# A diffusion backbone on one core: fetching each weight twice in place of splitting a raw copy

## The chip, the cores and the metric

The kernel runs on one core of a Trainium2 chip. The metric is device microseconds of one execution, the median of three runs; a profiled execution, recorded apart from these, gives the trace. TensorE (PE) multiplies matrices, VectorE (DVE), ScalarE (ACT) and GpSimd (POOL) work elementwise, SyncE (SP) issues transfers here, and 16 DMA engines carry them.

## The reference

Two layers over 256 context tokens and 256 latent tokens, 1024 channels, all in float32. Each layer is two normalised sub-layers with modulation: three parallel token mixers, then a gated MLP.

```python
def layer(x, ctx):                       # cut to what matters here
    u = rms_norm(x) * (1 + scale) + shift
    u_A, u_B, u_C, u_G = split_cols(u @ w_in)
    y = [rwkv7_branch(u_A), rglru_branch(u_B), na_branch(u_C)]
    m = sum(sigmoid(u_G[i]) * (y[i] @ w_branch[i]) for i in range(3))
    x = x + gate * rms_norm(m @ w_out)
    h = modulate(rms_norm(x))
    g, v = split(h @ ffn_w_in)
    return x + gate2 * rms_norm((silu(dwconv3(g)) * v) @ ffn_w_out)
```

Branch A is a recurrence (RWKV-7, in both directions), B a linear recurrence with gates, C attention in a neighbourhood. The second layer needs the outputs of the latent tokens alone.

## The kernel before

The tokens lie along the free axis, 512 of them (or 256 in the second layer's products of latent tokens), the channels in tiles of 128 on the partitions. Every large matrix product is made of three: operands are split into a high part, rounded to float32r, and a low part that holds the rest, and `mm3` (L240) adds high x high, low x high and high x low for each 128 x 128 block of the weight (L246, L247, L248).

A weight is a [128, 1024] tile, 512 KB (some of `ffn_w_out` have 768 columns). `wload` (L217) fetches it and splits it: a DMA from SP's queue into `wr` (L222), a ScalarE copy that rounds it into the high part `wh` (L225), and a subtraction raw less high into the low part `wl` (L228), on VectorE or GpSimd as a table for each phase says (L226). There are 402 such weights in an execution. The main pool `wp` has three places for raw tiles and two for each part; a low-rank weight `lw` (L464) shares the places of the raw tiles. Merges and MLP add a second pool with one to three places of each kind, and `phase` (L211) sets how the weights rotate between the two.

The order of work: in each layer a mixer part of eight head pairs, in which the recurrence of one pair (L713 to L747) runs beside the projections (`proj`, L252) for the next and beside B and C; then the merge of the three branches (`merge_w`, L1103), the output projection, and the MLP (`ffn_in` and `out`). Some of the second half's products run by halves of the tokens, 256 columns each. A planner orders each engine's instructions when the program is built, by priority and by what is ready in its own model of time, and sets the semaphore waits; on the chip each engine's queue then runs in that order, so that an instruction that waits holds up what is behind it on its engine. GpSimd's share of the recurrence is the decay of the state (`r`, L732), the key scaling (`n`, L487) and other small steps.

Of the kernel before, what the change touches and what calls it, by code (L numbers as in the profile page):

```python
# [10 lines left out]
F32 = mybir.dt.float32  # L11
F32R = mybir.dt.float32r
# [7 lines left out]
P = 128  # L20
NTOK = 512
CT = 8
NCH = 8
# [28 lines left out]
# per layer: the order in which a head pair's parts are traced, their priorities, how the products of the other  # L52
# mixers are spread beside them, and which engine takes the work that several could take
# [104 lines left out]
class Net:  # L158
# [51 lines left out]
    # ---- weights: raw -> (hi, lo) in float32r  # L210
    def phase(self, l, name, wps=None):  # L211
        """From here on the weights rotate among wps; where their low parts are worked out: 1 for GpSimd."""
        self.lo, self.wn = CFG[l]["lo"][name], 0
        if wps:
            self.wps, self.wi = wps, 0

    def wload(self, ap, kt):  # L217
        nc = self.nc
        pool = self.wps[self.wi % len(self.wps)]
        self.wi += 1  # L220
        raw = pool.tile([P, 1024], F32, tag="wr", name="wr", bufs=3 if pool is self.wp else None)[:, :kt * P]
        nc.sync.dma_start(raw, ap)  # L222
        hi = pool.tile([P, 1024], F32R, tag="wh", name="wh")[:, :kt * P]
        lo = pool.tile([P, 1024], F32R, tag="wl", name="wl")[:, :kt * P]
        nc.scalar.activation(hi, raw, AF.Copy)  # L225
        eng = nc.gpsimd if self.lo[self.wn % len(self.lo)] else nc.vector  # L226
        self.wn += 1
        eng.tensor_tensor(lo, raw, hi.bitcast(F32), op=ALU.subtract)  # L228
        return hi, lo
# [35 lines left out]
    # ---- rms statistics of the tokens a ... b - 1: acc holds the sums of squares over the channel tiles  # L265
# [15 lines left out]
    def stat(self, st, sq, a, b, first, last):  # L281
        """Adds the sums of sq over its channels to st, a column for 128 tokens."""
# [13 lines left out]
    # ---- conditioning vectors of a layer: mod[128, 48, 2]  # L296
# [16 lines left out]
    def ada_chunk(self, l, n, kind="c"):  # L313
        """Columns 512 n ... 512 n + 511 of the modulation, four column groups side by side on TensorE."""
# [22 lines left out]
        # modulation: h = x rstd (ng (1 + sc)) + sh ; x += (g ng) o rstd  # L337
# [12 lines left out]
    def layer_consts(self, l):  # L350
# [19 lines left out]
        # softplus(-lam) = max(-lam, 0) + log1p(exp(-|lam|)); log1p(u) = 2 atanh(u / (2 + u))  # L370
# [53 lines left out]
    # ---- A: RWKV-7  # L424
# [16 lines left out]
    def rw_start(self, Q):  # L441
# [4 lines left out]
        # stacked over the partitions: (hi, lo) of w, (lo, hi) of a  # L446
# [14 lines left out]
    def rw_key(self, R, Q, p, n0):  # L461
        nc = self.nc
        T2 = self.rw_t2(R, Q)
        lw = self.wp.tile([P, 1024], F32, tag="wr", name="lw", bufs=3)[:, :640]  # L464
# [12 lines left out]
        # normalised key  # L477
# [93 lines left out]
    def rw_gram(self, R, u, n0):  # L571
        nc = self.nc
        KR, BK = u["KR"], u["BK"]
        G = R.tile([P, 2, 2, 2, NCH, 64], F32, tag="Gm", name="Gm")  # part, d, h, c
# [22 lines left out]
    def rw_rows(self, R, u, n0):  # L597
# [3 lines left out]
        # from here on [beta; k] decayed to the end of its chunk  # L601
# [3 lines left out]
        # value rows by token, for both directions  # L605
# [12 lines left out]
        # rows by token of [beta; k]  # L618
# [13 lines left out]
    def rw_inv(self, R, u):  # L632
# [9 lines left out]
        if self.cfg['f1']:  # L642
            # the block beside them makes room for the rows of keys
# [10 lines left out]
        # columns s of the inverse: rows 0-63 hold the odd ones, rows 64-127 the even ones, both in the even places  # L654
# [16 lines left out]
    def rw_inv2(self, R, u):  # L671
# [4 lines left out]
        T1 = Ap  # rows 0-31: T11, rows 96-127: Q  # L676
# [134 lines left out]
    # ---- B: RG-LRU  # L811
# [16 lines left out]
    def lru_gates(self, B, u, d):  # L828
# [4 lines left out]
        if self.cfg['lq']:  # L833
            # the parts of the products lie where the second direction's values come
# [54 lines left out]
    # ---- C: neighbourhood attention  # L889
    def softmax(self, C, ps, nk):  # L890
        """ps: list of PSUM views [128, nk] (same width); returns normalised probabilities in SBUF."""
# [22 lines left out]
    def attn_qkv(self, C, p, n0):  # L914
# [13 lines left out]
        # values: 4 windows of 4 rows by 32 columns, then the context  # L928
# [8 lines left out]
    def attn_pre(self, C, u, n0):  # L937
        nc = self.nc
        q, k, vw = u["q"], u["k"], u["vw"]
        # queries by blocks (n, r, c): rotated, then plain  # L940
# [8 lines left out]
        if self.cfg['sq']:  # L949
            # (hi, lo) of a head's plain queries over the partitions, the high parts in the head's own half; the  # L950
            # high parts of the context's keys in both halves, the low ones beside each other
# [24 lines left out]
        # value rows by token: 4 windows, then 2 context tiles  # L976
# [9 lines left out]
    def attn_stages(self, C, u, n0):  # L986
        """The products of the attention in an order in which each finds its operands ready when
        other products stand between."""
# [68 lines left out]
    def attn_o(self, C, u, w, lat):  # L1057
        """Both heads side by side on TensorE's columns."""
# [32 lines left out]
    # ---- merging  # L1091
# [13 lines left out]
    def merge_w(self, M, tiles, ths, x, first, n0, ada=()):  # L1105
        """M += (1 + tanh(u_g / 2)) (y @ w) of a branch, twice the gated product."""
# [16 lines left out]
    def resid(self, S, l, o, acc, s, a, b, src, dst):  # L1123
        """x += gg * o * rstd(o) in the place of o; writes x to dst, and returns the sums of its squares."""
# [18 lines left out]
    def mixers(self, l, n0, src):  # L1143
# [7 lines left out]
        with ExitStack() as es:  # L1151
# [7 lines left out]
            with tc.high_priority(offset=30000):  # L1159
                if n0:  # L1160
                    # the products of the latent tokens alone go first
                    self.rw_gl(R, n0)
                    for _ in range(ng[0] - fg):
                        self.gate(B, next(gates), n0)
# [22 lines left out]
            for p in range(CT):  # L1187
# [3 lines left out]
                for o in order:  # L1191
# [11 lines left out]
                    with ExitStack() as z:  # L1203
                        if o == "A":
                            z.enter_context(tc.high_priority(offset=early))
                        # z: the pair whose recurrence is to come (the next one after T when nothing is left)
# [68 lines left out]
            # two branches merge beside the last head pair's recurrence, in the places of tiles done with  # L1275
# [42 lines left out]
    def btiles(B, n0):  # L1318
        """Tiles hi, lo of the 8 channel tiles in the places of the branches' tiles."""
# [275 lines left out]
```

## Time and profile before

| what | us |
|---|---|
| median of three runs | 3066.45 |
| lowest and highest | 3055.29, 3069.74 |
| span of the profiled execution, first to last instruction | 3050.6 |
| TensorE busy | 2886.2 (95%) |
| VectorE busy | 1968.9 (65%) |
| ScalarE busy | 1411.1 (46%) |
| GpSimd busy | 840.6 (28%) |

The span is shorter than the time of a run, since what lies before the first and after the last instruction isn't in it; the profiled execution has no time of its own beside its span. A matmul's record is longer than its step in the pipeline, so TensorE's busy time joins overlapping records. Busy time is a mean over very different parts of the kernel, which is why the stretches are read one by one.

### The profile page before, as it was taken

What the parts mean: (1) busy time and instruction counts of PE and PEld (TensorE: products, weight loads), DVE (VectorE), ACT (ScalarE), POOL (GpSimd) and SP (SyncE); (2) the same over time, 40 slices, a digit from 0 to 9 for tenths busy, and PEclk for the clock granted to TensorE, in tenths of its full rate; (3) what the DMA queues carried; (4) which work ended last, traced back from release to release, by engine and by line L of the source; (5) the groups of instructions that cost most, each with busy time, mean ns of one, the idle gap of its engine ahead of it and who ended that gap; (6) DMA issues with size and microseconds to landing.
All of it is one profiled execution on the core that took longest, in us unless ns stands there. A gap on an engine that the chain in (4) does not pass through costs nothing. (4 is left out here: it accounts for less than half of the span.)

```text
span 3050.6 us, 53179 instructions
## 1 busy us (share of the span) xinstructions
PE 2886.2 (95%) x21104; PEld 2265.9 (74%) x21104; DVE 1968.9 (65%) x3745; ACT 1411.1 (46%) x2485; POOL 840.6 (28%) x788
## 2 busy tenths in 40 slices
PE   7999999999999999999999998998999999998998
PEld 5666776766767678687778886776776777788898
DVE  6757658576686653465444267788677778775784
ACT  4454455554455452253323245454554545554553
POOL 3341322424234225100000113433432433414220
PEclk9999999999999899998999998998988999999899
DMA  6222122211222225755562352222222122245653
GB/s 229 81 70 67 59 71 66 74 60 56 69 76 70 84 100 180 273 190 180 198 223 92 107 183 82 62 78 69 68 72 69 62 70 78 77 140 205 222 188 115
DMA packets 130553, 344.39 MB, mean 113 GB/s; under 512 B 14720, under 2 KB 41600, under 8 KB 130304
## 3 DMA queue, kind: packets, MB, share of 16 engines
q1 hardware_dynamic: 123392, 334.69, 33.1%
q10 hardware_dynamic: 6912, 6.29, 0.7%
q8 instruction: 166, 2.72, 0.4%
q14 instruction: 83, 0.68, 0.1%
HBM read 301.08 MB, written 25.17 MB: 107 GB/s over the span
## 5 line engine op out<-in xcount | busy, mean ns | idle before, releaser
L225 ACT ACTIVATE wh<-wr 128x1024 fp32r<-128x1024 f32 (+1 forms) x402 | 420.8, 1048 | 581.0 <-PE pj L247 209.1
L248 PE MATMUL pj<-hh,wl 128*128 128x512 f32 (+1 forms) x1440 | 559.0, 389 | 41.4 <-DVE wl L228 40.0
L246 PE MATMUL pj<-hh,wh 128*128 128x512 f32 (+1 forms) x1440 | 569.7, 397 | 5.8 <-ACT gt L1088 3.0
L228 DVE TENSOR_TENSOR wl<-wr,wh 128x1024 fp32r<-128x1024 f32 (+1 forms) x310 | 398.2, 1285 | 266.5 <-ACT wh L225 244.2
L247 PE MATMUL pj<-hl,wh 128*128 128x512 f32 (+1 forms) x1440 | 556.0, 386 | 0.0
L228 POOL TENSOR_TENSOR wl<-wr,wh 128x1024 fp32r<-128x1024 f32 (+1 forms) x92 | 221.1, 2403 | 637.1 <-ACT wh L225 343.6
L248 PEld LDWEIGHTS pj<-hh,wl 128*128 128x128 f32 x1440 | 280.7, 195 | 104.6 <-DVE wl L228 45.7
L246 PEld LDWEIGHTS pj<-hh,wh 128*128 128x128 f32 x1440 | 280.6, 195 | 70.0 <-issue 16.4
L247 PEld LDWEIGHTS pj<-hl,wh 128*128 128x128 f32 x1440 | 280.4, 195 | 55.1 <-issue 13.4
L666 DVE TENSOR_TENSOR AT<-AT,itmp 128x126 f32<-128x126 f32 (+22 forms) x496 | 154.7, 312 | 11.8
L732 POOL TENSOR_TENSOR r<-SV,gC 64x256 f32<-64x256 f32 x96 | 84.2, 877 | 242.0 <-DVE SV L745 139.8
L664 DVE TENSOR_TENSOR itmp<-AT 128x126 f32<-128x126 f32 (+22 forms) x496 | 138.1, 278 | 12.0
L585 PEld LDWEIGHTS gram<-KR,BK 64*128 64x128 f32 x1024 | 116.3, 193 | 27.4 <-ACT Gm L590 14.8
L585 PE MATMUL gram<-KR,BK 64*128 64x128 f32 (+1 forms) x1024 | 131.3, 288 | 4.9 <-ACT Gm L590 4.7
L246 PE MATMUL fo<-fh,wh 128*128 128x256 f32 (+1 forms) x418 | 131.0, 313 | 0.0
L248 PE MATMUL fo<-fh,wl 128*128 128x256 f32 (+1 forms) x418 | 130.7, 313 | 0.0
L247 PE MATMUL fo<-fl,wh 128*128 128x256 f32 (+1 forms) x418 | 130.4, 312 | 0.0
L246 PE MATMUL fu<-hh,wh 128*128 128x256 f32 (+1 forms) x384 | 126.2, 330 | 3.1 <-DVE fgs L1347 2.4
L246 PE MATMUL fg<-hh,wh 128*128 128x256 f32 (+1 forms) x384 | 127.2, 333 | 0.1
L248 PE MATMUL fu<-hh,wl 128*128 128x256 f32 (+1 forms) x384 | 126.4, 330 | 0.8 <-DVE wl L228 0.8
L247 PE MATMUL fg<-hl,wh 128*128 128x256 f32 (+1 forms) x384 | 126.0, 330 | 0.0
L247 PE MATMUL fu<-hl,wh 128*128 128x256 f32 (+1 forms) x384 | 125.8, 328 | 0.0
(344 smaller groups left out, 6481.6 us busy)
## 6 DMA issues: line engine op xcount, KB each, us to landing
wr<-in_w_in SPq DMA_DIRECT2D x180, 512.0 KB, 3.2
aw<-in_ada_w SPq DMA_DIRECT2D x96, 512.0 KB, 4.4
wr<-in_ffn_w_in SPq DMA_DIRECT2D x96, 512.0 KB, 3.4
wr<-in_w_branch SPq DMA_DIRECT2D x48, 512.0 KB, 3.3
wr<-in_ffn_w_out SPq DMA_DIRECT2D x36, 512.0 KB, 3.5
wr<-in_w_out SPq DMA_DIRECT2D x24, 512.0 KB, 4.4
Gm<-KR SPq DMA_DIRECT2D x32, 256.0 KB, 3.6
wr<-in_ffn_w_out SPq DMA_DIRECT2D x18, 384.0 KB, 3.1
```

Source lines behind the costliest of these rows:

```text
L225: nc.scalar.activation(hi, raw, AF.Copy)
L228: eng.tensor_tensor(lo, raw, hi.bitcast(F32), op=ALU.subtract)
L246: nc.tensor.matmul(o, lhsT=a, rhs=xh[k][:, n0:n1], start=(first and k == 0), stop=False)
L247: nc.tensor.matmul(o, lhsT=a, rhs=xl[k][:, n0:n1], start=False, stop=False)
L248: m = nc.tensor.matmul(o, lhsT=b, rhs=xh[k][:, n0:n1], start=False, stop=(last and k == kt - 1))
L585: nc.tensor.matmul(ps[:, i, 0:nx], lhsT=BK[hs, d, c, :], rhs=KR[hs, 0:nx, d, c, :], start=True, stop=True)
L664: eng.tensor_tensor(tmp, Ap[:, q + 1:32, q:q + 1].to_broadcast([P, nt, ns]), Tf[:, q:q + 1, 0:2 * ns:2].to_broadcast([P, nt, ns]), op=ALU. ...
L666: eng.tensor_tensor(Tf[:, q + 1:32, 0:2 * ns:2], Tf[:, q + 1:32, 0:2 * ns:2], tmp, op=ALU.subtract)
L732: nc.gpsimd.tensor_tensor(sg, S0, gcb, op=ALU.mult)
```

## The change

`wload` holds no raw tile. The high part comes straight from DRAM by a transfer that GpSimd issues and that rounds to float32r on the way. ScalarE then writes the high part's negative into the low part's tile, and a second transfer, issued by GpSimd as well, adds the whole weight from DRAM to it. The subtraction on VectorE or GpSimd is gone. The main pool has three places for each part in place of two, the other pools as many as before; the low-rank tile has one place in place of three. All else in the diff removes comments.

```diff
     def wload(self, ap, kt):
         nc = self.nc
         pool = self.wps[self.wi % len(self.wps)]
         self.wi += 1
-        raw = pool.tile([P, 1024], F32, tag="wr", name="wr", bufs=3 if pool is self.wp else None)[:, :kt * P]
-        nc.sync.dma_start(raw, ap)
-        hi = pool.tile([P, 1024], F32R, tag="wh", name="wh")[:, :kt * P]
-        lo = pool.tile([P, 1024], F32R, tag="wl", name="wl")[:, :kt * P]
-        nc.scalar.activation(hi, raw, AF.Copy)
-        eng = nc.gpsimd if self.lo[self.wn % len(self.lo)] else nc.vector
-        self.wn += 1
-        eng.tensor_tensor(lo, raw, hi.bitcast(F32), op=ALU.subtract)
+        hi = pool.tile([P, 1024], F32R, tag="wh", name="wh", bufs=3 if pool is self.wp else None)[:, :kt * P]
+        lo = pool.tile([P, 1024], F32R, tag="wl", name="wl", bufs=3 if pool is self.wp else None)[:, :kt * P]
+        nc.gpsimd.dma_start(hi, ap)
+        nc.scalar.activation(lo, hi.bitcast(F32), AF.Copy, scale=-1.0)
+        nc.gpsimd.dma_start(lo, ap, accum_op=ALU.add)
         return hi, lo
...
     def rw_key(self, R, Q, p, n0):
-        lw = self.wp.tile([P, 1024], F32, tag="wr", name="lw", bufs=3)[:, :640]
+        lw = self.wp.tile([P, 1024], F32, tag="wr", name="lw", bufs=1)[:, :640]
```

## Rows read from the trace of the kernel before

**Rows 1.** Page, busy us, share of the span and instructions of each engine.
```profile
PE 2886.2 (95%) x21104; PEld 2265.9 (74%) x21104; DVE 1968.9 (65%) x3745; ACT 1411.1 (46%) x2485; POOL 840.6 (28%) x788
```

**Rows 2.** Page, 40 equal slices: granted clock in tenths, GB/s moved.
```profile
PEclk9999999999999899998999998998988999999899
GB/s 229 81 70 67 59 71 66 74 60 56 69 76 70 84 100 180 273 190 180 198 223 92 107 183 82 62 78 69 68 72 69 62 70 78 77 140 205 222 188 115
```

**Rows 3.** Busy time by stretch: start:end, length, engines, clock, DMA share, GB/s.
```profile
core 0: us, PE busy (x) PEld busy (x) DVE busy (x) ACT busy (x) POOL busy (x), PEclk, DMA share, GB/s
0.00:1130.00 1130.00, 1074.33 (x7584) 770.74 (x7585) 745.37 (x1612) 542.11 (x1012) 348.85 (x348) 0.97 0.24 81
1130.00:1296.00 166.00, 160.33 (x950) 122.79 (x951) 66.71 (x75) 50.21 (x68) 59.59 (x33) 0.98 0.65 224
1296.00:1417.00 121.00, 110.63 (x933) 103.99 (x928) 79.14 (x150) 63.24 (x116) 6.00 (x5) 0.93 0.58 197
1417.00:1740.00 323.00, 320.47 (x1990) 250.69 (x1991) 130.15 (x168) 98.08 (x133) 11.58 (x6) 1.00 0.46 153
1740.00:1805.00 65.00, 62.86 (x510) 61.48 (x508) 38.54 (x71) 31.75 (x58) 14.91 (x9) 0.97 0.55 178
1860.00:2690.00 830.00, 775.67 (x6033) 597.07 (x6033) 646.06 (x1273) 430.23 (x781) 306.04 (x320) 0.93 0.23 72
2735.00:2800.00 65.00, 58.38 (x468) 57.98 (x467) 39.45 (x52) 27.17 (x37) 20.64 (x19) 0.95 0.70 240
2850.00:2975.00 125.00, 125.00 (x1079) 124.33 (x1078) 104.16 (x144) 74.12 (x114) 36.48 (x15) 1.00 0.62 205
2975.00:3050.60 75.60, 63.35 (x533) 62.81 (x531) 32.77 (x47) 25.82 (x38) 0.69 (x1) 0.93 0.38 115
```

**Rows 4.** The same stretches, ScalarE's passes into `wh` alone (x is their number).
```profile
0.00:1130.00 1130.00, 95.15 (x90) 0.97 0.24 81
1130.00:1296.00 166.00, 28.49 (x28) 0.98 0.65 224
1296.00:1417.00 121.00, 30.58 (x29) 0.93 0.58 197
1417.00:1740.00 323.00, 55.97 (x54) 1.00 0.46 153
1740.00:1805.00 65.00, 17.14 (x17) 0.97 0.55 178
1860.00:2690.00 830.00, 81.36 (x77) 0.93 0.23 72
2735.00:2800.00 65.00, 21.94 (x21) 0.95 0.70 240
2850.00:2975.00 125.00, 48.21 (x47) 1.00 0.62 205
2975.00:3050.60 75.60, 19.47 (x20) 0.93 0.38 115
```

**Rows 5.** TensorE's waits, 1860 to 2690: us in total, times, longest.
```profile
PE pj L248 <- DVE wl L228: 40.0, 9, 7.4
PE r L720 <- DVE SV L745: 8.5, 7, 1.6
```

**Rows 6.** Page, costliest groups: the split of a weight (busy, mean ns, idle before).
```profile
L225 ACT ACTIVATE wh<-wr 128x1024 fp32r<-128x1024 f32 (+1 forms) x402 | 420.8, 1048 | 581.0 <-PE pj L247 209.1
L228 DVE TENSOR_TENSOR wl<-wr,wh 128x1024 fp32r<-128x1024 f32 (+1 forms) x310 | 398.2, 1285 | 266.5 <-ACT wh L225 244.2
L228 POOL TENSOR_TENSOR wl<-wr,wh 128x1024 fp32r<-128x1024 f32 (+1 forms) x92 | 221.1, 2403 | 637.1 <-ACT wh L225 343.6
```

**Rows 7.** Page, DMA issues: number, KB each, median us from issue to landing.
```profile
wr<-in_ffn_w_in SPq DMA_DIRECT2D x96, 512.0 KB, 3.4
```

**Rows 8.** Tile `wr` on SP's queue: ns min/median/max of one issue.
```profile
L222 SPq DMA_DIRECT2D wr<-in_ffn_w_in x96: 327/328/940, 1325.4 to 2947.7; - x96
```

**Rows 9.** Subtractions into `wl`, 1860 to 2690: on VectorE, then on GpSimd.
```profile
1860.00:2690.00 830.00, 69.30 (x54) 0.93 0.23 72
1860.00:2690.00 830.00, 54.98 (x23) 0.93 0.23 72
```

## The prediction, made before the changed kernel was run

> **What bounds the kernel now.** I read the busy line of the page first: TensorE works 95% of the span, VectorE 65%, ScalarE 46%, GpSimd 28% [rows 1]. So at most 164 us (3050.6 less 2886.2) can be won without taking work off TensorE, and the change takes none off it. Then the clock and DMA lines [rows 2]: the clock is near its 2.4 GHz level nearly everywhere, and DMA runs at 60 to 80 GB/s in the two long mixer parts but at 180 to 270 GB/s in humps around slices 15 to 21 and at the end. Then the stretches [rows 3] beside the number of weights (one ScalarE pass each) that they take [rows 4]. Two regimes are to be seen there:
> - Mixers, 0 to 1130 and 1860 to 2690 us: one weight per 12.6 and per 10.8 us, DMA share 0.24 and 0.23. Here TensorE loses 56 and 54 us, and VectorE is busy 745 and 646 us.
> - Merges and MLP: one weight per 2.7 to 6 us, DMA share 0.46 to 0.70, TensorE nearly full.
> Last the waits of TensorE [rows 5]: in the second mixer part 40.0 us of its idle time are for the low part of a weight from VectorE, in 9 waits; the next largest is 8.5 us. That is the only large wait that the change aims at.
>
> **Part 1, what goes.** 310 VectorE and 92 GpSimd subtractions of 1.29 and 2.40 us [rows 6], that is 398 and 221 us of engine time. Neither engine bounds a stage by its busy time (VectorE at most 104 of 125 us, 83%, [rows 3]), so the worth is what TensorE waits for them: the 40 us of [rows 5], and a little of the other VectorE waits. I put the gain at 40 us, bound 0 (the same weights then wait for something else) and 60 us (those 40 and the 8.5 of the recurrence, and as much again in the first mixer part, where I saw no such wait). SP no longer issues 402 weights at 0.33 us each [rows 8]; nobody waits for SP's issue time itself, so nothing is booked. Dropping two of three places of the small low-rank tile costs nothing: one is used per head pair, eight pairs in 1130 us, so its place is free long before.
>
> **Part 2, what stays.** The ScalarE pass remains, now as a negation of the same 128x1024 elements: 1.05 us as before [rows 6]. ScalarE gains nothing. What moves is its position: it now waits for the first transfer to land, where the raw copy had mostly landed early.
>
> **Part 3, what is added: bytes.** Each of the 402 weights is fetched twice. Price of one 512 KB transfer in engine time of all 16 DMA engines: in 2735 to 2800 us a share of 0.70 of 65 us moved 240 GB/s x 65 us = 15.6 MB, so 1.53 us per 512 KB; in 1417 to 1740 us likewise 0.46 x 323 = 148.6 us for 49.4 MB, 1.58 us [rows 3]. Call it 1.55 us. The first transfer takes the place of the raw one at that price (a rounding transfer isn't in the trace; bound: from the same up to the accumulating one's). The second is new and has no row either. Below: a plain copy, 1.55 us. Above: it has to read two operands, source and destination, for each result, so two copies, 3.1 us. I take 2.3 us, three passes over memory (two reads and a write) against a copy's two. Then the DMA time of each stretch, share x length + weights x price, against its length [rows 3, 4]:
> 1130-1296: 107.9 + 28 x 2.3 = 172 against 166, over by 6.
> 1296-1417: 70.2 + 29 x 2.3 = 137 against 121, over by 16.
> 1417-1740: 148.6 + 54 x 2.3 = 273 against 323, fits.
> 1740-1805: 35.8 + 17 x 2.3 = 75 against 65, over by 10.
> 2735-2800: 45.5 + 21 x 2.3 = 94 against 65, over by 29.
> 2850-2975: 77.5 + 47 x 2.3 = 186 against 125, over by 61.
> 2975-3050: 28.7 + 20 x 2.1 (smaller tiles) = 71 against the 62 in which the products run, over by 9.
> Sum +131 us. With 1.55 us it is +38 (13 and 25 in the two stretches of the second layer), with 3.1 us +260.
>
> The Trainium skill (Collectives: The Full Stack, section The bandwidth ceiling) says that an add in the DMA path costs no arithmetic time but reads two sources through one read ring, so that it moves at half a copy's rate. By that rule the second transfer would cost two copies and this sum +260; no run so far shows one.
>
> **Part 4, what is added: latency and places.** Before, a weight needed one landing of about 3.4 us [rows 7], a ScalarE and a VectorE pass, with three raw places ahead of two pairs. Now a place is held for landing 3.4, negation 1.05, second landing 3.4 to 5 and two issues on GpSimd. An issue from GpSimd isn't in the trace: below 0.33 us as on SP [rows 8], above 2.4 us as its pass over 1024 columns [rows 6]; I take 1.0. Together 3.4 + 1.05 + 4.2 + 2 = 10.6 us, plus the products, 2.66 us a weight at 256 columns where TensorE is full (125 us for 47 in 2850 to 2975 us, [rows 3, 4]): a place turns round in 13.3 us. With the three places of the main pool alone that is 4.4 us a weight, with five 2.7, with six 2.2. In the last MLP (six places, 2.66 us a weight) that stays behind the DMA bound; in 1740-1805 (three and one place, 3.3 to 4.4 us a weight against 3.8 now) and 2735-2800 (first half three places) it is about as large as the DMA bound, not on top of it. I book nothing beyond Part 3, and 10 us at the start, where the first weights now come through two landings with nothing to hide behind.
>
> **Part 5, what is added: waits on GpSimd and ScalarE.** GpSimd now issues 804 transfers, 2.0 us per weight against 2.4 us for the 92 it had. In the second mixer part that is 77 x 2.0 = 154 us in place of the 55 us of 23 subtractions [rows 9], GpSimd 306 to some 405 of 830 us. Each first issue waits for TensorE to leave the place, each second for ScalarE; queued behind are GpSimd's steps of the recurrence (the decay multiplies, key scaling), for which TensorE, VectorE and the next step wait. On ScalarE the negation waits for a landing, and the evictions of the recurrence are queued behind. If all 77 weights held a queue on the chain for one us, it is +77; if the order has them ready, 0. I take +60 for both mixer parts together, nearer to the upper end since GpSimd's 0.33-to-2.4 us price is open too.
>
> **Sum.** -40 + 131 + 10 + 60 = +161 us on the profiled execution. Its span is 3050.6 us; the runs give 3055.29 to 3069.74, median 3066.45, so 5 to 19 us lie around it and stay. 3066 + 161 = 3227; I say 3230.
>
> **Rivals.**
> A. The second transfer costs two copies or the rounding one is dearer as well: +260 in place of +131 and somewhat more waiting, 3066 + 260 + 10 + 100 - 40 = about 3400. For it: two operands are read. Against: the share counts time in packets, in which reading may overlap writing.
> B. GpSimd serves a weight strictly in sequence: issue, landing 3.4, negation 1.05, issue, then the next. That is 6.5 us per weight, and it decides wherever weights come faster, as in all seven dense stretches (216 weights in 941 us, 4.4 us each [rows 3, 4]): 216 x 6.5 = 1404, +463 us, with the other terms about 3550. Against: the issue of a later weight has only a place to wait for, and the planner may put it first.
> C. Faster: VectorE bounds the second mixer part more than its waits show (646 of 830 us, 78%), and shedding its 54 subtractions there [rows 9] shortens the chain of the recurrence by more than 40 us, while DMA overlaps both transfers at a copy's price or below: -80 + 38 = about 3025. It decides if the DMA engines move above 400 GB/s; the fullest slice shows 273 [rows 2].
> D. No change: gains of 40 to 60 against +38 with the cheap price, about 3066.
> E. The transfers don't round or add as meant: the same time, no case of its own.
>
> **How the numbers follow.** The forecast 0.46 (3110 to 3320), A 0.22, B 0.12, C 0.13, D 0.07. A change under 0.5% (15 us) can't be told from none here: faster 0.13, same 0.07, slower 0.80. The range leaves out B and the outer half of C and reaches into A beyond its time: 3045 to 3450.
>
> **What will show it.** Right: TensorE's idle time grows in 2735 to 3050 and its waits there name the second transfer; the DMA share in the last MLP goes to 0.9 or more; VectorE falls to about 1570 us. Wrong on size: a second transfer's landing well off 4 to 5 us. B would show TensorE starved with DMA below 0.7 and GpSimd's queue waiting for ScalarE. C would show the second mixer part shorter than 830 us and DMA above 350 GB/s. If TensorE idles much, its granted clock may fall toward 1.2 GHz, as it did to 0.93 in 1296-1417 [rows 3]; that would lengthen the stretches with waits further.

## The result

The changed kernel takes 3579.71 us (median of four runs, 3570.80 to 3593.01) against 3060.87 us for the kernel before on the same chip: 1.1695 times as long, 95% interval 1.1652 to 1.1738. The forecast was 3230 us, with a range up to 3450. So the direction was right and the loss, 519 us, three times the 161 us of the sum. The profiled execution's span is 3591.0 us, 540 us more than before. That execution took 3593.01 us, the slowest of the four, and where both are known the span is about 2 us below the time. By that the 3050.6 us of before belong to its fastest execution (3052.03 us), and lengths by span overstate the loss by some 20 us.

The page of the changed kernel, in the order of [rows 1, 2]: busy time, then granted clock, DMA share and GB/s in 40 slices, then the two DMA queues that carry weights (q0 is GpSimd's, new; q1 is SP's): packets, MB, share of the 16 engines' span.

```profile
PE 3092.6 (86%) x21104; PEld 2428.5 (68%) x21104; DVE 1502.9 (42%) x3435; ACT 1417.0 (39%) x2485; POOL 1152.3 (32%) x1500
...
PEclk9999999899999989788899978899998899777888
DMA  7545444454454788896776776546455556698998
GB/s 226 117 108 111 95 110 98 102 114 92 102 123 108 206 218 245 217 235 167 191 179 148 162 190 147 119 107 135 111 118 111 115 125 146 159 230 215 233 226 196
...
q0 software_dynamic: 115776, 416.86, 52.2%
q1 hardware_dynamic: 65504, 126.26, 10.9%
```

TensorE runs the same 21104 products, but is busy 206 us longer, at a lower granted clock (mean 0.897 against 0.959), and idle 334 us longer. VectorE lost 466 us of work, 398 of them the subtractions of [rows 6]. The DMA engines are at 0.8 or more in the merges and the last MLP, yet at little over 200 GB/s, less than the 240 GB/s that a share of 0.70 moved before [rows 3].

The new work, from the page's groups (busy, mean ns | idle before, and its main cause) and from its list of transfers (median us from issue to landing):

```profile
L225 ACT ACTIVATE wl<-wh 128x1024 fp32r<-128x1024 f32 (+1 forms) x402 | 419.6, 1045 | 790.6 <-DMA wh<-in_w_in 201.8
...
L226 POOL DMA_DIRECT2D wl<-in_ffn_w_in x96 | 83.7, 886 | 388.4 <-ACT wl L225 276.4
...
wh<-in_ffn_w_in POOLq DMA_DIRECT2D x96, 512.0 KB, 8.0
wl<-in_ffn_w_in POOLq DMA_DIRECT2D x96, 512.0 KB, 6.6
```

Two landings of 8.0 and 6.6 us stand where one of 3.4 us stood [rows 7], and GpSimd sits before the second issue waiting for ScalarE, which waits for the first landing. TensorE's waits, whole run (us in total, times, longest), end there, and at the conditioning weights `aw`, which come through the same engines:

```profile
PE fo L246 <- DMA wl<-in_ffn_w_out: 63.3, 18, 6.3
PE pbr L246 <- DMA wl<-in_w_branch: 46.5, 20, 4.5
PE ada L324 <- DMA aw<-in_ada_w: 46.4, 20, 4.7
PE fg L246 <- DMA wl<-in_ffn_w_in: 40.7, 14, 4.6
```

To compare runs I cut each at the same pieces of work: the first product of a branch merge (`pbr`), the first and last product of the gate half of `ffn_w_in` (`fg`), the last with `ffn_w_out` (`fo`), in each layer; 0 and 1 are the layers, and the last column runs to the end of the span. Lengths in us, from the starts of those products:

| | mixers 0 | merges 0 | MLP in 0 | MLP out 0 | mixers 1 | merges 1 | MLP in 1 | MLP out 1 |
|---|---|---|---|---|---|---|---|---|
| before | 1136.5 | 213.1 | 305.7 | 136.9 | 899.2 | 153.8 | 126.3 | 79.1 |
| changed | 1195.7 | 289.0 | 427.2 | 200.5 | 924.3 | 245.8 | 193.5 | 115.0 |
| longer by | 59 | 76 | 122 | 64 | 25 | 92 | 67 | 36 |

The stretches of the changed kernel, columns as in [rows 3]:

```profile
0.00:1195.70 1195.70, 1108.07 (x7612) 793.65 (x7613) 657.12 (x1543) 546.95 (x1018) 426.92 (x514) 0.94 0.49 116
1195.70:1484.70 289.00, 233.42 (x1386) 184.12 (x1384) 55.96 (x110) 78.58 (x123) 80.35 (x100) 0.89 0.88 234
1484.70:1911.90 427.20, 335.89 (x2074) 267.89 (x2075) 93.77 (x181) 108.69 (x159) 74.85 (x106) 0.86 0.74 191
1911.90:2112.40 200.50, 152.16 (x793) 130.88 (x792) 21.80 (x52) 48.34 (x74) 46.20 (x65) 0.87 0.73 159
2112.40:3036.70 924.30, 856.98 (x6444) 674.57 (x6442) 565.25 (x1278) 467.12 (x842) 363.09 (x491) 0.92 0.56 127
3036.70:3282.50 245.80, 179.11 (x1212) 156.65 (x1212) 44.62 (x123) 69.05 (x121) 72.11 (x100) 0.76 0.83 202
3282.50:3476.00 193.50, 148.49 (x1034) 144.61 (x1035) 52.71 (x119) 69.37 (x109) 57.01 (x81) 0.86 0.91 219
3476.00:3591.00 115.00, 78.48 (x558) 76.17 (x557) 11.64 (x29) 28.90 (x42) 31.80 (x44) 0.86 0.85 207
```

Merges and MLPs lost 457 of the 540 us. In some the DMA engines are nearly full (0.88, 0.91), in the first layer's MLP they are not (0.74, 0.73), and TensorE starves all the same. What GpSimd's queue does differs between the two. Its timeline (start, us, instruction, count, idle before and its end) first in the first layer's MLP, then in the last:

```profile
1708.29 0.85 POOL L226 DMA_DIRECT2D wl<-in_ffn_w_in  x1 [5.27 <-ACT wl L225]
1709.03 0.67 POOL L224 DMA_DIRECT2D wh<-in_ffn_w_in  x1
1719.05 0.86 POOL L226 DMA_DIRECT2D wl<-in_ffn_w_in  x1 [9.35 <-ACT wl L225]
1723.80 0.55 POOL L224 DMA_DIRECT2D wh<-in_ffn_w_in  x1 [3.89 <-PE fg L246]
1730.97 0.85 POOL L226 DMA_DIRECT2D wl<-in_ffn_w_in  x1 [6.63 <-ACT fh L231]
...
3313.76 0.88 POOL L226 DMA_DIRECT2D wl<-in_ffn_w_in  x1 [8.28 <-ACT wl L225]
3315.17 0.87 POOL L226 DMA_DIRECT2D wl<-in_ffn_w_in  x1 [0.52 <-ACT wl L225]
3316.71 0.86 POOL L226 DMA_DIRECT2D wl<-in_ffn_w_in  x1 [0.67 <-ACT wl L225]
3317.24 1.95 POOL L224 DMA_DIRECT2D wh<-in_ffn_w_in  x3
3327.14 0.88 POOL L226 DMA_DIRECT2D wl<-in_ffn_w_in  x1 [7.94 <-ACT wl L225]
```

In the first it alternates: a second transfer of one weight, the first of the next, and then it waits for that one to land and be negated, or for TensorE to leave a place (3.89 us at 1723.80). In the last it goes in threes, a turn taking 13.4 us (3313.76 to 3327.14), 4.5 us a weight. The DMA lines of 3300 to 3345 us, 40 slices of 1.1 us, show what the engines do in these turns:

```profile
DMA  0799999999992299999999994879999999994779
GB/s 33 70 204 186 219 218 164 200 259 415 419 390 69 29 146 215 197 200 215 211 197 397 419 430 149 66 98 208 204 204 208 215 222 397 415 419 135 80 127 222
```

Each turn is six to seven slices at about 207 GB/s (three adding transfers), then three to four at about 415 GB/s (three rounding ones), then two or three nearly empty. So an addition takes the engines twice as long as a rounding copy there, and on top of it they stand still while the chain turns.

### The profile page after: what moved, and what is told of

It reads as the page before. It is cut to its first block, busy times and chain, and to the rows that moved or that the text cites. A ratio compares the mean times of both kernels' runs of the same rounds, so it can differ in the third digit from the quotient of the medians.

```text
span 3591.0 us, 53564 instructions
## 1 busy us (share of the span) xinstructions
PE 3092.6 (86%) x21104; PEld 2428.5 (68%) x21104; DVE 1502.9 (42%) x3435; ACT 1417.0 (39%) x2485; POOL 1152.3 (32%) x1500
## 4 chain that ended last, share of the span: by engine, by line
PE 24%; issue 19%; DMA 13%; POOL 7%; DVE 2%; ACT 1%; POOLq 0%; ACTq 0%; DVEq 0%; SPq 0%
POOL wl L226 3%; POOL wh L224 2%; PE pj L245 2%; DMA wh<-in_ffn_w_in 2%; PE pj L246 2%; PE pj L244 2%; DMA aw<-in_ada_w 2%; DMA wl<-in_ffn_w_in 1%; DMA wl<-in_w_in 1%; DMA wl<-in_w_branch 1%; PE gram L583 1%; DMA wh<-in_ffn_w_out 1%; PE r L718 1%; PE pbr L246 1%; PE sa L733 1%
## 5 line engine op out<-in xcount | busy, mean ns | idle before, releaser
L225 ACT ACTIVATE wl<-wh 128x1024 fp32r<-128x1024 f32 (+1 forms) x402 | 419.6, 1045 | 790.6 <-DMA wh<-in_w_in 201.8
L246 PE MATMUL pj<-hh,wl 128*128 128x512 f32 (+1 forms) x1440 | 562.9, 391 | 37.6 <-DMA wl<-in_w_in 37.6
L245 PE MATMUL pj<-hl,wh 128*128 128x512 f32 (+1 forms) x1440 | 571.5, 398 | 0.1
L246 PEld LDWEIGHTS pj<-hh,wl 128*128 128x128 f32 x1440 | 287.1, 199 | 95.5 <-DMA wl<-in_w_in 42.1
L226 POOL DMA_DIRECT2D wl<-in_w_in x180 | 160.6, 894 | 400.6 <-ACT wl L225 365.6
L224 POOL DMA_DIRECT2D wh<-in_w_in x180 | 111.6, 620 | 353.8 <-PE pj L246 266.2
L226 POOL DMA_DIRECT2D wl<-in_ffn_w_in x96 | 83.7, 886 | 388.4 <-ACT wl L225 276.4
L246 PE MATMUL fo<-fh,wl 128*128 128x256 f32 (+1 forms) x418 | 141.9, 342 | 63.3 <-DMA wl<-in_ffn_w_out 63.3
L246 PE MATMUL fg<-hh,wl 128*128 128x256 f32 (+1 forms) x384 | 142.3, 371 | 40.7 <-DMA wl<-in_ffn_w_in 40.7
L246 PE MATMUL fu<-hh,wl 128*128 128x256 f32 (+1 forms) x384 | 137.5, 358 | 40.0 <-DMA wl<-in_ffn_w_in 40.0
L583 PE MATMUL gram<-KR,BK 64*128 64x128 f32 (+1 forms) x1024 | 150.0, 317 | 11.5 <-ACT Gm L588 11.3
L583 PEld LDWEIGHTS gram<-KR,BK 64*128 64x128 f32 x1024 | 133.6, 220 | 34.4 <-ACT Gm L588 20.5
L664 DVE TENSOR_TENSOR AT<-AT,itmp 128x126 f32<-128x126 f32 (+22 forms) x496 | 135.2, 273 | 12.3
L246 PEld LDWEIGHTS fo<-fh,wl 128*128 128x128 f32 x418 | 88.4, 212 | 73.2 <-DMA wl<-in_ffn_w_out 68.2
```

Of the source, the lines that this page charges most:

```text
L224: nc.gpsimd.dma_start(hi, ap)
L225: nc.scalar.activation(lo, hi.bitcast(F32), AF.Copy, scale=-1.0)
L226: nc.gpsimd.dma_start(lo, ap, accum_op=ALU.add)
L245: nc.tensor.matmul(o, lhsT=a, rhs=xl[k][:, n0:n1], start=False, stop=False)
L246: m = nc.tensor.matmul(o, lhsT=b, rhs=xh[k][:, n0:n1], start=False, stop=(last and k == kt - 1))
L583: nc.tensor.matmul(ps[:, i, 0:nx], lhsT=BK[hs, d, c, :], rhs=KR[hs, 0:nx, d, c, :], start=True, stop=True)
```

## The experiments

Two theories. **DMA price**: the second transfer costs about twice a copy, and merges and MLPs run at the pace of the 16 engines. **Chain**: a weight's place is held through landing, negation and landing, in queues that run in order, and that turn sets the pace. Runs named e_ edit the changed kernel, runs named b_ the kernel before. Spans and stages below are of the profiled executions, one for each kernel, set against the kernel before; lengths in us. Executions of one kernel lie up to 29 us apart (3283.35 and 3312.11 us for e_plain), which goes for the sizes below too.

### The two halves of the loss

**e_plain**, the second transfer a copy:

```diff
-        nc.gpsimd.dma_start(lo, ap, accum_op=ALU.add)
+        nc.gpsimd.dma_start(lo, ap)
```

> The second transfer is a rounding copy like the first, not an addition, so the low part is wrong; order, waits and bytes from DRAM are those of the changed kernel. Theory DMA price (an accumulating transfer takes the 16 DMA engines twice as long as a rounding one, 2.5 against 1.25 us per 512 KB, and the merges and MLPs run at that pace): about 1.27 us less per weight wherever the DMA share was 0.84 or more, some 130 weights, so 3580 - 165 = about 3415 us, and the last MLP's part (3282 to 3577 us in the changed kernel) shrinks from 295 to about 210 us. Theory chain (a place is held through two landings and a negation, and GpSimd's queue waits between): only the second landing gets shorter, about 1.3 of 8.5 us per turn, so 15% of the excess of 520 us goes: about 3500 us.

Measured 3297.73 us, 1.076 (1.064 to 1.0879).

**e_nochain**, the negation reads a constant:

```diff
-        nc.scalar.activation(lo, hi.bitcast(F32), AF.Copy, scale=-1.0)
+        ones = self.smask[:, :kt * 64].rearrange("p (o b) -> p o b", o=1).to_broadcast([P, 2, kt * 64])
+        nc.scalar.activation(lo.rearrange("p (o b) -> p o b", o=2), ones, AF.Copy, scale=-1.0)
```

> ScalarE writes minus one (from a constant) into the low part in place of the negated high part, so the low part is wrong; nothing waits for the first transfer's landing any more, while transfers, their kinds and bytes, GpSimd's issues, ScalarE's work and the places are those of the changed kernel. Theory DMA price: the merges and MLPs stay where they are, 3580 us less at most 40. Theory chain: the 512-column part of the first layer's MLP (8.3 us per weight) goes back towards the 6.0 us it had, and the last MLP loses the gaps between its batches of transfers (4.4 to 3.8 us per weight): about 3580 - 110 - 45 - 40 (merges) = 3385 us.

Measured 3331.81 us, 1.0871 (1.0827 to 1.0915). The landings got no shorter: for `ffn_w_in` the medians are 7.9 and 10.0 us, against 8.0 and 6.6 us in the changed kernel. What went is the wait for the first one. In its last MLP the DMA engines no longer pause; 3110 to 3155 us in 40 slices, and GpSimd's queue in that window:

```profile
DMA  9999999999999999999999999999999999999999
GB/s 222 277 364 222 233 368 262 211 339 302 229 280 339 244 226 390 240 211 350 288 233 277 342 240 237 368 255 222 328 302 226 280 350 240 237 357 262 218 342 295
DMA packets 3454, 12.61 MB, mean 280 GB/s; under 512 B 382, under 2 KB 382, under 8 KB 3452
...
q0 software_dynamic: 3452, 12.58, 108.4%
```

A mean of 280 GB/s, so two transfers of 0.524 MB in 3.75 us; that stage takes 156.0 us for 44 weights, 3.5 us each. There the price is all that is left. A share of 108.4% also says that the times of packets overlap: a share is not the part of the time in which the engines are taken up.

**e_both**, both edits at once:

> The changed kernel with both earlier cuts: the second transfer is a rounding copy and ScalarE's pass doesn't wait for the first one's landing (the low part is wrong). Bytes from DRAM are still doubled and GpSimd still issues both. If the price of the accumulating transfer and the chain are all of the loss, this is at the kernel before, 3050 to 3090 us. If doubled bytes cost by themselves, the merges and the last MLP stay 20 to 30 us longer each: 3110 to 3160 us.

Measured 3130.34 us, 1.0223 (1.017 to 1.0276). TensorE's longest wait over the whole run is then for the conditioning weights:

```profile
PE ada L325 <- DMA aw<-in_ada_w: 45.8, 27, 4.2
```

**e_nosecond**, no second transfer:

```diff
-        nc.gpsimd.dma_start(lo, ap, accum_op=ALU.add)
```

> No second transfer: the low part is the negated high part, which is wrong; the rest is as in the changed kernel. Theory DMA price: one rounding transfer per weight costs less than the raw one did, so every stretch fits: 3060 to 3100 us, less if the unburdened VectorE gains anything. Theory chain: a place is held 6 to 7 us shorter, so also near 3100; if the wait of ScalarE for a landing and GpSimd's issues alone cost much, it stays above 3200.

Measured 3088.99 us, 1.0084 (1.0055 to 1.0113), where both theories had it, so it doesn't tell them apart.

The growth of the span over before, and by stage:

| run | span | mixers 0 | merges 0 | MLP in 0 | MLP out 0 | mixers 1 | merges 1 | MLP in 1 | MLP out 1 |
|---|---|---|---|---|---|---|---|---|---|
| changed | +540 | 59 | 76 | 122 | 64 | 25 | 92 | 67 | 36 |
| e_nochain | +279 | -2 | 55 | 80 | 24 | 3 | 66 | 30 | 22 |
| e_plain | +231 | 20 | 46 | 48 | 35 | -11 | 41 | 32 | 20 |
| e_both | +74 | -10 | 24 | 29 | 13 | -8 | 28 | -3 | 1 |
| e_nosecond | +36 | 0 | 21 | 23 | 2 | -12 | 1 | 0 | 0 |

Neither theory is enough alone, and each cut gave back more than either theory had said. Taking the price away is worth 309 us with the chain and 205 us without it; taking the chain away is worth 261 us with the price and 157 us without it. So the two together cost about 104 us more than the sum of each alone. By the medians of the runs, each set against the kernel before on its chip, the four figures are 285, 203, 250 and 169 us, and 82 us on top; with e_plain's interval of 37 us to either side the size of this last term is rough. It fits that a dear transfer lengthens the landings of which the chain has two: for `ffn_w_in` they are 8.0 and 6.6 us with the addition, 6.0 and 4.6 us as copies (e_plain). What is left with neither, doubled bytes at a copy's price and GpSimd's issues, less what VectorE's relief brings, costs 74 us, none of it in the last MLP.

### What the price is

**e_halfacc**, the addition on half of the columns:

```diff
-        nc.gpsimd.dma_start(lo, ap, accum_op=ALU.add)
+        nc.gpsimd.dma_start(lo[:, :kt * 64], ap[:, :kt * 64], accum_op=ALU.add)
```

> The changed kernel with the second transfer adding only the first half of each weight's columns (the low part is wrong in the other half). If the engine time of the accumulating bytes is what it costs, 256 KB that are added take as long as 512 KB that are copied, and this stands near the run with a plain second transfer: 3280 to 3330 us. If a fixed cost of each accumulating transfer (its issue on GpSimd, its landing) does, it stays above 3450 us.

Measured 3370.23 us, 1.1025 (1.0985 to 1.1066). GpSimd's DMA queue (packets, MB, share) on the pages of e_nosecond, e_plain and e_halfacc, one fence each:

```profile
q0 software_dynamic: 57888, 208.43, 23.2%
```

```profile
q0 software_dynamic: 115776, 416.86, 41.9%
```

```profile
q0 software_dynamic: 115776, 312.66, 40.9%
```

Share times span gives the engine time. First transfers alone: 0.232 x 3086.6 = 716 us, 1.78 us each of 402. Both as copies: 0.419 x 3281.6 = 1375 us, so the second 1.64 us. Half added: 0.409 x 3369.8 = 1378 us, the second 1.65 us for 256 KB. All added (the changed kernel): 0.522 x 3591.0 = 1875 us, the second 2.88 us. This takes the first transfers to cost 1.78 us in every run, which wasn't measured; e_both and e_nochain give 1.58 and 2.86 us for the second in the same way. So adding 256 KB takes the engines as long as copying 512 KB, and most of the price goes by bytes; 2.88 us is less than twice 1.65 us, so a part of some 0.4 us for each transfer isn't excluded. Engine time isn't all of the difference either: the run lies between its two expectations, and with the same engine time e_halfacc takes 72 us longer than e_plain. Its longer issue on GpSimd (medians of 0.86 to 0.89 us, against 0.53 to 0.59 us) is one candidate, not tried by itself.

### What the chain is made of

**e_w2**, a second place in the first layer's MLP:

```diff
-            W = es.enter_context(tc.tile_pool(name="wf", bufs=1 if n0 == 0 else 3, reuse_waits="tile", side="right"))
+            W = es.enter_context(tc.tile_pool(name="wf", bufs=2 if n0 == 0 else 3, reuse_waits="tile", side="right"))
...
-        lw = self.wp.tile([P, 1024], F32, tag="wr", name="lw", bufs=1)[:, :640]
+        lw = self.wp.tile([P, 640], F32, tag="wr", name="lw", bufs=1)
```

> The changed kernel with two places in place of one for each part in the second weight pool of the first layer's MLP (room comes from cutting the low-rank tile to the 640 columns that it uses). Theory DMA price: the MLP of the first layer runs at the pace of the DMA engines or of TensorE already: within 20 us of 3580. Theory chain: that MLP (1475 to 2112 us) waits for the one place to turn round, so it shrinks by 60 to 120 us: about 3490.

Measured 3552.74 us, 1.1592 (1.1516 to 1.1667), 27 us below the changed kernel. By the profiled span it is 48 us shorter, 45 of them in that MLP (28 and 17 us in its parts), where 60 to 120 were expected. So the place is a part of it.

**e_wf5**, five places in place of three in the second layer's MLP:

```diff
-            W = es.enter_context(tc.tile_pool(name="wf", bufs=1 if n0 == 0 else 3, reuse_waits="tile", side="right"))
+            W = es.enter_context(tc.tile_pool(name="wf", bufs=1 if n0 == 0 else 5, reuse_waits="tile", side="right"))
```

> The changed kernel with five in place of three places for each part in the second weight pool of the second layer's MLP, eight with the main pool's. Theory chain (places too few for the two landings): that MLP, 4.4 us per weight in the changed kernel, goes to the 3.5 to 3.8 us that the DMA engines need; its two parts (193.5 and 115.0 us) shrink by 45 us together: about 3535 us. Theory DMA price alone, or GpSimd's queue alone (each waiting issue holds the next one): both parts stay within 10 us: 3570 to 3590 us.

Measured 3583.84 us, 1.1677 (1.1538 to 1.1817), no change in the median (24 us by span). The two parts take 181.4 and 115.0 us, 12 and 0 us less. Six places were not what held that MLP; GpSimd's queue still goes in groups with 5 to 8 us of waiting between them.

**e_hiprio**, first transfers ahead in the planner's order:

```diff
-        nc.gpsimd.dma_start(hi, ap)
+        with self.tc.high_priority(offset=2000):
+            nc.gpsimd.dma_start(hi, ap)
```

> The changed kernel with a higher priority for the first transfers when the planner orders GpSimd's queue, so that they come ahead of second ones that wait for a negation. If that order is what starves TensorE: 60 us or more below 3580. If the places are the limit, a first transfer can't start before a place is free, and it stays within 30 us of 3580.

Measured 3557.74 us, 1.1592 (1.1514 to 1.167): 22 us below, 35 by span. GpSimd's waits move from the second issue (for the negation, 893 to 773 us) to the first (for TensorE's products `fg` in the MLPs, 65 to 147 us): the places then hold it up instead.

**e_vneg**, the negation on VectorE:

```diff
-        nc.scalar.activation(lo, hi.bitcast(F32), AF.Copy, scale=-1.0)
+        nc.vector.tensor_scalar(lo, hi.bitcast(F32), -1.0, None, op0=ALU.mult)
```

> The changed kernel with the negation on VectorE in place of ScalarE, so that the wait for the first landing stands in VectorE's queue. If ScalarE's queue, held up by that wait, delays the evictions and the conditioning products behind it, merges and the first layer's MLP get shorter: 50 us or more below 3580. If the wait costs only through the place that it keeps, within 25 us of 3580, and the second layer's mixers lose some of what VectorE was relieved of (20 to 40 us).

Measured 3542.32 us, 1.1542 (1.1463 to 1.1621): 37 us below, 50 by span, between the two expectations; the first layer's MLP gains 24 us, merges 1 gain 22, and mixers 1 lose 5.

So no single link gives back more than 50 of the 261 us of span that cutting the chain does. That places, order and ScalarE's queue hold each other up, so that what one lets through the next stops, fits these runs and e_hiprio's waits; the links weren't loosened together, and which share each has stays open.

### What relief of VectorE is worth, and why it didn't come

**b_nosub**, the kernel before without the subtraction:

```diff
-        lo = pool.tile([P, 1024], F32R, tag="wl", name="wl")[:, :kt * P]
...
-        eng.tensor_tensor(lo, raw, hi.bitcast(F32), op=ALU.subtract)
-        return hi, lo
+        return hi, hi
```

> The kernel before without the subtraction: the high part stands in for the low one, so the result is wrong; transfers, ScalarE and TensorE have the same work. It measures the most that VectorE and GpSimd can give back. The prediction's first part says 40 us (bounds 0 and 60), in the second layer's mixers: 3020 us. The rival, that TensorE then waits for something else, says 3050 to 3060 us.

Measured 3007.10 us, 0.9821 (0.9769 to 0.9873), 58 us by the medians. The span is 41 us shorter, 40 of them in mixers 1. TensorE's longest waits there, 1800 to 2659 us, no longer name a weight:

```profile
PE Q L683 <- DVE AT L676: 22.9, 8, 4.4
PE pj L244 <- ACT gt L1086: 3.3, 2, 1.9
```

**b_swraw**, the kernel before with the raw transfer issued by GpSimd:

```diff
-        nc.sync.dma_start(raw, ap)
+        nc.gpsimd.dma_start(raw, ap)
```

> The kernel before with the raw weight's transfer issued by GpSimd in place of SP, everything else as it was: 402 issues on GpSimd's in-order queue, one plain transfer per weight. If GpSimd's queue order by itself holds up the recurrence or the weights, the mixers get 20 us or more longer: above 3090 us. If not: within 15 us of 3062 us.

Measured 3113.38 us, 1.0168 (1.0114 to 1.0222). It grows by 13 us in mixers 0, 21 in mixers 1, 8 and 14 in the merges, and not in the MLPs. GpSimd has 402 issues of 0.53 to 0.59 us (medians), and often waits before one for VectorE to be done with the raw tile's place (640 us in 187 times); the recurrence's steps are queued behind.

**b_mixacc**, the kernel before, with the low part by negation and an adding transfer from the raw tile in the mixers of the second layer, where it was on VectorE:

```diff
+        self.acc = l == 1 and name in ('st', '1', 'Q', 'N', 'X', 'Y', 'G')
...
-        eng.tensor_tensor(lo, raw, hi.bitcast(F32), op=ALU.subtract)
+        if self.acc and eng is nc.vector:
+            nc.scalar.activation(lo, hi.bitcast(F32), AF.Copy, scale=-1.0)
+            nc.gpsimd.dma_start(lo, raw, accum_op=ALU.add)
+        else:
+            eng.tensor_tensor(lo, raw, hi.bitcast(F32), op=ALU.subtract)
```

> The kernel before with its raw copy, and in the second layer's mixers alone the subtractions that stood on VectorE replaced: ScalarE negates the high part and a transfer that GpSimd issues adds the raw tile to it. So VectorE is relieved as in the changed kernel, but no weight waits for two landings from DRAM and the raw copy still comes early. If the chain and the bytes from DRAM ate the 40 us that the run without subtractions showed, most of it comes back here: 3025 to 3045 us. If GpSimd's queue and the accumulating transfer eat it by themselves: 3060 us or more.

Measured 3120.71 us, 1.0214 (1.0184 to 1.0245): mixers 1 are 74 us longer. TensorE's work and waits there, first the stretch before (1792 to 2691 us), then this run's, with two of its waits:

```profile
1792.00:2691.00 899.00, 837.65 (x6427) 650.17 (x6427) 688.00 (x1341) 464.71 (x838) 322.89 (x338) 0.94 0.24 78
1788.00:2761.00 973.00, 881.64 (x6489) 691.07 (x6487) 613.43 (x1299) 526.18 (x908) 346.13 (x402) 0.89 0.40 105
PE Q L690 <- DVE AT L683: 29.9, 8, 5.4
PE pj L253 <- DMA wl<-wr: 25.5, 14, 4.5
```

The wait for the low part that VectorE made (40.0 us, [rows 5]) is now one of 25.5 us for the transfer, and a wait in the recurrence has grown beside it, from 1.8 us; it stood at 22.9 us in b_nosub too. These waits aren't all: of the 74 us TensorE is busy for 44, for 1% more products, at a granted clock of 0.89 in place of 0.94.

**b_mixall**, the same without the condition on the engine:

```diff
-        if self.acc and eng is nc.vector:
+        if self.acc:
```

> As the run before it, with the subtractions that stood on GpSimd replaced too, so that GpSimd issues 77 or more accumulating transfers in the second layer's mixers in place of 23 subtractions of 2.4 us. If GpSimd's time matters there, it is 5 to 15 us faster than that run; if its queue's waits for ScalarE do, up to 20 us slower.

Measured 3079.46 us, 1.0077 (1.0046 to 1.0108): 41 us faster than b_mixacc, where 5 to 15 were expected, and still slower than before; mixers 1 are 15 us longer. Its mixers 0, in which nothing was edited, are 12 us longer all the same. The planner orders the whole program anew for each edit, and differences of a dozen us in one stage shouldn't be read as more than that.

### One part of the change alone

**b_round**, the high part by a rounding transfer, raw copy and subtraction kept:

```diff
-        nc.scalar.activation(hi, raw, AF.Copy)
+        nc.gpsimd.dma_start(hi, ap)
```

> The kernel before with one part of the change alone: the high part comes by a rounding transfer that GpSimd issues, in place of ScalarE's pass; the raw copy and the subtraction stay. Bytes doubled at a copy's price, no landing waits for another. Theory DMA price: two plain-priced transfers fit in most stretches, the last MLP (2.66 us per weight against about 2.5 to 3.3 us of DMA) is 0 to 30 us longer: 3060 to 3110 us. Theory chain: with no second landing behind a first, at or a little below the kernel before: 3030 to 3065 us.

Measured 3256.70 us, 1.0636 (1.0547 to 1.0725). Both expectations were too low: it grows by 51 us in merges 0, 41 in the first layer's MLP in, 36 in merges 1, 23 in mixers 1. It has the two places of the high part that the copy from a waiting raw tile needed, now for a transfer that lands in 5.0 us. **b_round3** gives it three, and two to the raw tile:

```diff
-        raw = pool.tile([P, 1024], F32, tag="wr", name="wr", bufs=3 if pool is self.wp else None)[:, :kt * P]
+        raw = pool.tile([P, 1024], F32, tag="wr", name="wr")[:, :kt * P]
...
-        hi = pool.tile([P, 1024], F32R, tag="wh", name="wh")[:, :kt * P]
+        hi = pool.tile([P, 1024], F32R, tag="wh", name="wh", bufs=3 if pool is self.wp else None)[:, :kt * P]
...
-        nc.scalar.activation(hi, raw, AF.Copy)
+        nc.gpsimd.dma_start(hi, ap)
...
-        lw = self.wp.tile([P, 1024], F32, tag="wr", name="lw", bufs=3)[:, :640]
+        lw = self.wp.tile([P, 1024], F32, tag="wr", name="lw")[:, :640]
```

> The earlier run with the high part by a rounding transfer beside the raw copy (3257 us), with three places for the high part and two for the raw tile in the main pool, in place of two and three; the room is the same. There the two places of the high part, which now must cover a landing, were to blame if this is 60 to 110 us faster (3150 to 3200 us). If doubled bytes or GpSimd's queue were, it stays at 3240 to 3270 us.

Measured 3330.59 us, 1.0852 (1.0776 to 1.0928), slower by 74 us, which neither expectation had. The merges of the first layer did as expected (51 us of growth fell to 16), but mixers 1 went from 23 to 125 us of growth. That stage in b_round, then in b_round3:

```profile
1906.90:2829.00 922.10, 846.33 (x6435) 662.40 (x6433) 676.86 (x1348) 381.60 (x755) 367.74 (x431) 0.93 0.42 128
1894.60:2918.40 1023.80, 922.08 (x6333) 712.21 (x6331) 649.74 (x1316) 381.37 (x756) 354.32 (x430) 0.83 0.38 115
```

Of the 102 us between them TensorE is idle for 26 and busy for 76, at a granted clock of 0.83 in place of 0.93. GpSimd's waits for TensorE to leave a place of `wh` in the projections rose as well, over the whole run from 353 to 423 us. Whether the clock, those waits or the raw tile's lost place came first wasn't separated. No version tried that computes the whole is faster than the kernel before.

## Why the prediction was wrong, point by point

**What bounds.** Right: merges and MLPs, the waits at the second transfer, a DMA share of 0.91 in the last MLP, VectorE near its forecast (1503 us for 1570). Mixers grew by 84 us where the terms outside Part 3 (-40, +10, +60) said 30.

**Part 1, the gain of 40 us.** The size and the place were right: b_nosub shows 41 us, 40 of them in mixers 1. The step that failed is to book it as a gain beside a separate cost. With VectorE relieved, mixers 1 are 25 us longer in the changed kernel, where TensorE waits for the second transfer in the place of the subtraction (`PE pj L246 <- DMA wl<-in_w_in: 31.5, 12, 3.7`), and without that transfer 12 us shorter, which is no more than the planner's noise.

**Part 2.** ScalarE's 1.05 us was right (1045 ns). That its new position matters was said and left without a price of its own; taking its wait for the landing away (e_nochain) is worth 261 us.

**Part 3, the price, sized too low.** I took 1.55 and 2.3 us, 3.85 for a weight. By the measure that the part used, share of time, GpSimd's queue gives 1.78 and 2.88 us, 4.66. That is the upper bound of the part, at which the sum said +260: the value chosen between the bounds failed, for three passes over memory against two was a count without a row. From a copy's price to 2.3 us the sum grew by 93 us (131 less 38), to two copies by 222; without the chain the runs put the price at 205 us (e_nochain less e_both). So in total the upper bound fits. By stage it fits in part only. For the products of the last MLP it gave 73 us (98 less 25) and the runs show 33 (30 and -3); for the first layer's MLP in it gave at most 39 us, all of 1296-1417 counted to it, and the runs show 51 (80 and 29). So the agreement of the totals is partly luck. Nor is the share a strict measure: in e_nochain's last MLP, where the engines are full, a weight takes 3.75 us by the bytes moved, close to the 3.85. The Trainium skill's rule (Collectives: The Full Stack, section The bandwidth ceiling), stated there for ReduceScatter, said two copies; the slices with 207 beside 415 GB/s agree, and over the whole run it is 2.88 to 1.64, 1.76 times. It was set down as a rival with 0.22.

**Part 4, the step that cost most.** Two errors. First the turn of a place: 10.6 us was made of landings of 3.4 and 4.2 us, with two issues on top. A landing is counted from the start of its issue; for `ffn_w_in` the turn is 8.0 + 1.05 + 6.6 = 15.7 us before any wait in a queue. Landings grow with the other transfers on the way: the first one takes 3.9 us in e_nosecond, 6.0 us in e_plain and 8.0 us here. Second, "about as large as the DMA bound, not on top of it": I took the larger of two bounds. Engines with pauses in each turn are at neither bound: the chain adds 157 us by itself, 261 us beside the price. In the first layer's MLP at 512 columns Part 3 found that the bytes fit, 273 against 323 us, and booked nothing; with the part at 256 columns before it, it became 122 us longer at a DMA share of 0.74.

**Part 5.** The order of GpSimd's queue was named, with 60 us for the mixers; b_swraw shows 34 us for the mixers from issuing one plain transfer per weight there, and 57 us over all. What the part left out is that the merges pay for it too (22 us); in b_swraw the MLPs don't.

**The rivals.** A had the price near what the runs show in total, and not the chain. B, strict sequence at 6.5 us a weight, describes the first layer's MLP (one second and one first issue in turn, some 11 to 12 us apart in the lines above), not the last, which goes in threes; its 3550 us came nearest by luck, through a sequence everywhere and no price of the bytes at all. The two were set apart as alternatives with 0.22 and 0.12, when nothing excluded that both hold. That is why the range ended 130 us short. C asked for more than 400 GB/s: rounding copies reach 415, but additions run at half of it, and mixers 1 got longer, not shorter.

**The clock.** The text said that a starving TensorE may lose clock. It did: 0.76 in merges 1 and 0.86 or 0.87 in the MLPs against 0.93 to 1.00 in [rows 3], and the same products kept it busy 206 us longer. How much of the 540 us this adds, rather than filling time that would have been idle, no run here separates; in b_round3's mixers 1, 76 of 102 us came as busy time at the lower clock.

## What to carry to other kernels

Before a step is moved from an engine to a transfer, price it as a link in a chain: landing under load, wait of the next engine, the queue behind that wait, and how many places cover the whole turn. Bounds that a work item passes in turn add up unless there are places enough to overlap them, and here cost some 80 to 100 us more than their sum, so the larger of two bounds is only the floor. And a wait that an engine's relief takes away is a gain only if what replaces the work is earlier in the same place; the run without the work shows the ceiling (here 41 us by span, 58 by the medians), the run with the replacement alone shows whether any is left.

## What the runs showed of the hardware

An adding transfer moved about 207 GB/s where a rounding one moved about 415, in neighbouring slices of one MLP and with the engines at nine tenths or more in both; by engine time over whole runs it is 2.88 against 1.64 us per transfer. An adding issue held GpSimd for 0.87 to 0.89 us (medians), a rounding or plain one for 0.53 to 0.59 us in the runs without additions; in the changed kernel's MLPs the rounding issues stand at 0.87 us, many of them right behind an adding one. A rounding transfer from GpSimd was a little dearer to the engines than a plain one: 1.78 us each in e_nosecond, against 0.209 x 3107.2 / 402 = 1.62 us for plain ones from the same queue in b_swraw, and 0.331 x 3050.6 = 1010 us for 334.7 MB before, 1.58 us per 512 KB from SP's; the load on the engines differs between these runs.
